# RWKV and mLSTM float32 products of 64 rows and 128 columns, cut into 64x64 quarters of the TensorE array

## The chip, the core and the metric

The kernel runs on one core of one Trainium2 chip. The metric is the device time of one execution in microseconds, less is better. A core has five engines that each work through their own instructions in order: TensorE (PE; its weight loads are listed as PEld), VectorE (DVE), ScalarE (ACT), GpSimd (POOL) and SyncE (SP, which issues the DMAs here).

TensorE multiplies a stationary operand (rows times columns of the array, at most 128x128) with a stream of columns. A product whose operands have 64 rows uses one row half of the array, and a result of 64 partitions one column half; the first is set by the partitions that the operands lie on, the second by the partitions of the result.

## The reference

The reference is a block of an RWKV-7 part beside an mLSTM part with a feed-forward part behind them, and then two layers of attention, on 1024 tokens of width 1024 in float32. The change touches the first block alone, cut here to what matters:

```python
def rwkv7_group(p, mu, w0, w_up_decay, a0, w_up_a, ...):
    ...
    log_w = -jax.nn.softplus(-(w0 + jnp.tanh(w_lo) @ w_up_decay)) - 0.5
    a = jax.nn.sigmoid(a0 + a_lo @ w_up_a)
    ...
    y = rwkv7_scan(r_h, heads(decay), k_h, v_h, -kk, kk * a_h)
    # per step: sa = S a_t;  S = S * w_t + sa b_t + v_t k_t;  y = S r_t

def mlstm_chunkwise(q, k, v, ig, logf):
    ...
    s = jnp.einsum('bhtd,bhsd->bhts', qc, kc) * d
    num = jnp.einsum('bhts,bhsv->bhtv', s, vc) + sc[..., None] * jnp.einsum('bhtd,bhdv->bhtv', qc, C)
    ...
    C = dec[..., None, None] * C + jnp.einsum('bhs,bhsd,bhsv->bhdv', w_s, kc, vc)
```

RWKV has 8 heads of 64 channels, the mLSTM 4 heads of 64 key channels and 128 value channels.

## The kernel before

Most of the time goes to the projections: products of 128 rows, 128 columns and a stream of 512 (`gemm`, `proj`, `out_half`), where each weight and each activation is split into a high and a low part (whi and wlo; act, and yh and yl) and three products are added. They are called the big products below. They run on TensorE from the start to the end, and the small work of RWKV and of the mLSTM is laid between them.

RWKV runs over 8 units of 128 tokens. Each unit has an element part (`rw_elem`), a preparation (`rw_prep`), a chain over two chunks of 64 tokens (`rw_chain`) and an output part (`rw_out`). Two heads share 128 partitions: head pair hp has one head on partitions 0 to 63 and the other on 64 to 127, H[0] and H[1] in the code.

- In `rw_elem` two up-projections with 64 rows (the weights lie in `wup`, the first on partitions 0 to 63, the second on 64 to 127) make four results of 128 partitions each, in a tile tagged e: uw from tw, and ua from L (tile ML).
- In `rw_prep` the products of BK (stationary) and AR (stream) make the score tiles. For each of two groups g two result tiles tagged m, `apm[0]` and `apm[1]`, are filled, one for each row half hh, with four products each. VectorE then masks them to AA and AM. From AA a triangular inverse is built up over levels: products GD with Y make Z (VectorE), products XD with Z and ZD with X make the next Y and X (ScalarE).
- In `rw_chain` the tile P takes 64x64 products of S, RH, UV with AR, TT, BT and AM.

The mLSTM runs over 8 blocks of 128 tokens (`ml_block`). The score products (K of a head stationary, Q the stream, both in the tile QK) go to pst and are multiplied with the decay DT to SD; the state products (Q stationary, the state C the stream) go to pq and are scaled by ScalarE to NUM. Both are done for i = 0 and 1, the row halves, with two products each; all these result tiles are tagged p. Blocks 0 to 3 take their tiles from a pool with one slot, blocks 4 to 7 from a pool with two (`psl` in `block1` and `rest`). The tiles m have two slots.

All products are issued by the helper `mm` (L186) and all transposes by `tr` (L189). The order on each engine is not that of the code: a scheduler lays it out when the program is built, by priorities and by when a slot of a pool is free. On top of that RWKV and mLSTM groups are tied to the big products. `collect` gathers a part's TensorE work into groups, a new one beginning after each instruction of another engine, and `pace` orders the last instruction of group i before the big product number start + i*n:

```python
    def pe(self, inst):
        if self.grp is not None:
            if self.brk:
                self.grp.append(inst)
```

For the mLSTM n is 12 in both halves (NM and NCC).

Of the kernel before, what the change touches and what calls it, by code (L numbers as in the profile page):

```python
# [17 lines left out]
ALU = mybir.AluOpType  # L18
# [12 lines left out]
NG = 6  # L31
PA = 56, 1, 48, 1
BF, BL = 0, 100
CDEC = -0.5 * math.exp(-0.5)


# [92 lines left out]
class Kern:  # L129
# [562 lines left out]
    def rwkv(self, R, gR, gK, gV, gL, yd):  # L692
# [14 lines left out]
        k["cdec"] = self.t(rc, [128, 1], "cdec")  # L707
        nc.vector.memset(k["cdec"], CDEC)
        k["ka"] = self.t(rc, [128, 8], "ka")
# [59 lines left out]
    def rw_elem(self, R, u, gR, gK, gV, gL):  # L769
        nc = self.nc  # L770
        re, r2, r3, pe_ = R["re"], R["r2"], R["r3"], R["pse"]
        kc = self.rk
        gp = nc.gpsimd
        t0 = 128 * u

        def load(g, M):
            nc.sync.dma_start(M, g[:, :, t0:t0 + 128])

        L = self.t(re, [128, 2, 128], "ML")
        load(gL, L)  # L780
        tw = self.t(re, [64, 128], "tw")
        self.act(tw, L[0:64, 0], AF.Tanh)
        sg = self.t(r3, [128, 128], "sg")
        self.act(sg, L[:, 1], AF.Tanh, scale=0.5)
        self.ts(sg, sg, 0.5, 0.5)
        CUM = self.t(re, [128, 4, 128], "CUM")
        A = self.t(re, [128, 4, 128], "A")
        uw = self.t(pe_, [128, 4, 128], "e")
        for hp in range(4):
            self.mm(uw[:, hp], kc["wup"][0:64, hp * 128:hp * 128 + 128], tw)  # L790
        for hp in range(4):
            self.act(CUM[:, hp], uw[:, hp], AF.Tanh, bias=kc["wa0"][:, hp:hp + 1], scale=0.5)
        ua = self.t(pe_, [128, 4, 128], "e")
        for hp in range(4):
            self.mm(ua[:, hp], kc["wup"][64:128, hp * 128:hp * 128 + 128], L[64:128, 0])
        for hp in range(4):
            self.act(A[:, hp], ua[:, hp], AF.Tanh, bias=kc["wa0"][:, 4 + hp:5 + hp], scale=0.5)
        cdec = CDEC
        lw = self.t(re, [128, 4, 128], "t1")
        self.act(lw, CUM, AF.Identity, bias=kc["cdec"], scale=cdec)  # L800
        fl = lambda x: x.rearrange("p a b -> p (a b)")
        nc.vector.tensor_tensor_scan(fl(CUM), fl(kc["msk"]), fl(lw), 0.0, op0=ALU.mult, op1=ALU.add)
        ch = lambda x: x.rearrange("p a (c t) -> p a c t", t=64)
        E1 = self.t(re, [128, 4, 2, 65], "E1")
        nc.vector.memset(E1[:, :, :, 0:1], 1.0)
        self.act(E1[:, :, :, 1:65], ch(CUM), AF.Exp)
        EN = CUM
        self.act(EN, CUM, AF.Exp, scale=-1.0)
        EC = self.t(r3, [128, 2, 4], "EC")
        nc.vector.tensor_copy(EC.rearrange("p c a -> p a c"), E1[:, :, :, 64])  # L810
        Kx = self.t(re, [128, 4, 128], "MK", bufs=2)
        load(gK, Kx)
        KA = self.t(re, [128, 4, 128], "KA")
        SQ = self.t(re, [128, 4, 128], "t1")
        for hp in range(4):
            self.act(KA[:, hp], Kx[:, hp], scale=self.par("k_k", hp))
        self.act(SQ, KA, AF.Square)
        ss = self.t(pe_, [128, 512], "e")
        for hp in range(4):
            self.mm(ss[:, 2 * hp:2 * hp + 2], SQ[:, hp], kc["hsel"])  # L820
        sv = self.t(re, [128, 8], "sv")
        self.ts(sv, ss[:, 0:8], 1e-24, op0=ALU.max)
        rn = self.rsqrt(re, sv, "rn")
        rnb = self.t(re, [128, 8, 64], "t1")
        self.act(rnb, rn[:, :, None].to_broadcast([128, 8, 64]))
        bc = self.t(pe_, [128, 4, 128], "e")
        for hp in range(4):
            self.tr(bc[:, hp], rnb[:, 2 * hp:2 * hp + 2].rearrange("p a b -> p (a b)"), self.ident)
        self.tt(KA, KA, bc)
        AR = self.t(r2, [128, 4, 2, 128], "AR")  # L830
        BK = self.t(re, [128, 4, 4, 64], "BK")
        self.tt(AR[:, :, :, 0:64], ch(KA), E1[:, :, :, 0:64])

        self.stt(KA, A, 1.0, KA, op0=ALU.add, op1=ALU.mult)
        self.stt(BK[:, :, 1:3, :], ch(KA), -0.5, ch(EN), op0=ALU.mult, op1=ALU.mult)
        K2 = self.t(re, [128, 4, 128], "t1")
        for hp in range(4):
            self.act(K2[:, hp], A[:, hp], AF.Identity, bias=kc["ka"][:, 4 + hp:5 + hp], scale=kc["ka"][:, hp:hp + 1])
        self.tt(K2, K2, Kx)
        self.tt(BK[:, :, 0:4:3, :], ch(K2), ch(EN), eng=gp)  # L840
        Rx = self.t(re, [128, 4, 128], "MK", bufs=2)
        load(gR, Rx)
        self.tt(AR[:, :, :, 64:128], ch(Rx), E1[:, :, :, 1:65], eng=gp)
        V = self.t(re, [128, 4, 128], "V")
        load(gV, V)
        RK = A
        for hp in range(4):
            self.act(RK[:, hp], Rx[:, hp], scale=self.par("r_k", hp))
        self.tt(RK, RK, K2)
        bp = self.t(pe_, [128, 4, 128], "e")  # L850
        self.mm(fl(bp), kc["bones"], fl(RK))
        BON = self.t(r3, [128, 4, 128], "BON")
        self.tt(BON, bp, V)
        return dict(AR=AR, BK=BK, V=V, BON=BON, EC=EC, sg=sg)

    def rw_prep(self, R, U):

        nc = self.nc
        rx, r2, psm = R["rx"], R["r2"], R["psm"]
        kc = self.rk  # L860
        gp = nc.gpsimd
        AR, BK, V = U["AR"], U["BK"], U["V"]
        am = kc["am"]
        H = [slice(0, 64), slice(64, 128)]
        fl2 = lambda x: x.rearrange("p a b -> p (a b)")
        AA = self.t(rx, [128, 8, 2, 64], "AA")
        AM = self.t(r2, [128, 8, 2, 64], "AM")
        for g in range(2):
            apm = [self.t(psm, [128, 4, 128], "m") for _ in range(2)]
            for h2 in range(2):  # L870
                for c in range(2):
                    for hh in range(2):
                        self.mm(apm[hh][:, h2 * 2 + c], fl2(BK[H[hh], 2 * g + h2, 2 * c:2 * c + 2, :]),
                                AR[H[hh], 2 * g + h2, c, :])
            for T_, o in ((AA, 0), (AM, 64)):
                for hh in range(2):
                    h0 = hh * 4 + 2 * g
                    self.tt(T_[:, h0:h0 + 2].rearrange("p a c t -> p (a c) t"), apm[hh][:, :, o:o + 64],
                            am[:, None, o:o + 64].to_broadcast([128, 4, 64]))
# [47 lines left out]
        for h in range(8):  # L927
            hh, hp = h // 4, h % 4
# [217 lines left out]
    def ml_block(self, tb, mc, mx, my, psm, G, gQ, gW, gO, yd):  # L1146
        nc = self.nc
        bmd, TK, DEC, trik = (G[n] for n in ("bmd", "TK", "DEC", "trik"))
        C = G["C"]
        t0 = tb * 128  # L1150
        ts_ = slice(t0, t0 + 128)
        QK = self.t(my, [128, 4, 128], "QK")
# [14 lines left out]
        DT = self.t(mx, [128, 4, 128], "DT")  # L1167
# [6 lines left out]
        for j in range(2):  # L1174
# [2 lines left out]
        self.tt(KW, pk.rearrange("p j (h d) -> p (j h) d", d=64),  # L1177
                TK[:, tb, 1, :, None].to_broadcast([128, 4, 64]))
        SD = self.t(mx, [128, 4, 128], "SD")
        for i in range(2):  # L1180
            pr = slice(i * 64, i * 64 + 64)
            pst = self.t(psm, [128, 2, 128], "p")
            for h2 in range(2):
                self.mm(pst[:, h2], QK[pr, 2 + h2], QK[pr, h2])
            self.stt(SD[:, i:4:2], pst, 0.125, DT[:, i:4:2], op0=ALU.mult, op1=ALU.mult)
        NUM = self.t(mx, [128, 4, 130], "NUM")
        for i in range(2):
            pr = slice(i * 64, i * 64 + 64)
            pq = self.t(psm, [128, 2, 130], "p")
            for h2 in range(2):  # L1190
                self.mm(pq[:, h2, 0:129], QK[pr, h2], C[pr, h2, 0:129])
            for h2 in range(2):
                h = h2 * 2 + i
                self.act(NUM[:, h, 0:129], pq[:, h2, 0:129], scale=TK[:, tb, 3, h:h + 1])
        Cn = self.t(mc, [128, 2, 130], "C", bufs=2)
        pcs = self.t(psm, [128, 2, 130], "p")
        for h in range(4):
            h2, i = h // 2, h % 2
            self.mm(pcs[i * 64:i * 64 + 64, h2, 0:129], KW[:, h], V1[:, h, 0:129])
        for h in range(4):  # L1200
            h2, i = h // 2, h % 2
            pr = slice(i * 64, i * 64 + 64)
            self.stt(Cn[pr, h2, 0:129], C[pr, h2, 0:129], DEC[pr, h, tb:tb + 1], pcs[pr, h2, 0:129])
        for h2 in range(2):
            pn = self.t(psm, [128, 2, 130], "p")
            for i in range(2):
                self.mm(pn[:, i, 0:129], SD[:, h2 * 2 + i], V1[:, h2 * 2 + i, 0:129])
            self.tt(NUM[:, 2 * h2:2 * h2 + 2, 0:129], NUM[:, 2 * h2:2 * h2 + 2, 0:129], pn[:, :, 0:129], ALU.add)
        G["C"] = Cn

        den = self.t(mx, [128, 4, 1], "den")
        self.stt(den, NUM[:, :, 128:129], -1.0, NUM[:, :, 128:129], op0=ALU.mult, op1=ALU.max)
        self.tt(den, den, TK[:, tb, 2, :, None], ALU.max)
        nc.vector.reciprocal(den, den)
        HN = self.t(mx, [128, 4, 128], "HN")
        self.tt(HN, NUM[:, :, 0:128], den.to_broadcast([128, 4, 128]))
        SQ = self.t(mx, [128, 4, 128], "th")
# [7 lines left out]
        for h in range(4):  # L1225
            self.tr(ph[:, h], HN[:, h], self.ident)
        YO = self.t(mx, [128, 4, 128], "SD")
        for h in range(4):
# [488 lines left out]
```

## Time and profile before

| | |
|---|---|
| time, median of 3 runs | 3477.56 us (3473.36 to 3477.97) |
| time of the profiled execution | 3473.78 us |
| its span | 3471.8 us |
| TensorE busy | 3364.5 us, 97% of the span |
| mean granted TensorE clock | 0.989 |
| VectorE, ScalarE, GpSimd busy | 59%, 46%, 20% |

The span runs from the first to the last instruction of the profiled execution. Busy times of matrix products are unions of instructions that overlap in the pipeline, so the time from one start to the next tells more than the duration of one. In the timeline a row is a run of equal instructions: its start, the time from its start to the end of its last instruction, and the count. A float32 product of one row in the instruction order is two passes in the trace, and a transpose is one.

### The profile page before, as it was taken

Reading aid. Unit: us, or ns where it says so; the run is one execution under the profiler, and the core shown is the slowest. Engines: PE = TensorE matmul, PEld = TensorE weight load, DVE = VectorE, ACT = ScalarE, POOL = GpSimd, SP = SyncE. Lnnn points to the kernel's source line nnn. Section 1 sums busy time; section 2 is a strip of 40 time slices with the busy share of each in tenths; the row PEclk is TensorE's granted clock in tenths of the full one; section 3 lists DMA queues with packets and bytes.
Section 4 is the critical chain, followed back from the end, with each engine's and each line's share of the span. In section 5 each row is a group of like instructions: output and inputs, shape, how many; then the busy total and the mean of one; then the engine's idle time right before and its main releaser. Section 6 shows DMA issues by size and latency. Waiting matters only on the chain.

```text
span 3471.8 us, 51104 instructions
## 1 busy us (share of the span) xinstructions
PE 3364.5 (97%) x18820; PEld 2720.0 (78%) x18820; DVE 2043.1 (59%) x4223; ACT 1607.7 (46%) x3242; POOL 703.4 (20%) x601
## 2 busy tenths in 40 slices
PE   8999999989999999999999999999999999999998
PEld 6777777767777777778888878888778888788886
DVE  7777767656655754577666762224777567712335
ACT  5477766654433433345555652123355556621232
POOL 2212222222222222241111111111321111111111
PEclk9999999999999999999999999999999999999999
DMA  5433232223333323332212122113432121211124
GB/s 159 155 119 106 92 112 77 64 81 103 113 106 96 124 93 92 93 118 84 59 50 64 54 78 64 44 49 121 153 92 58 50 64 50 81 59 52 50 74 140
DMA packets 196986, 303.51 MB, mean 87 GB/s; under 512 B 22976, under 2 KB 65600, under 8 KB 196736
## 3 DMA queue, kind: packets, MB, share of 16 engines
q1 hardware_dynamic: 196736, 300.25, 28.0%
q8 instruction: 148, 2.42, 0.3%
q14 instruction: 102, 0.84, 0.1%
HBM read 244.41 MB, written 38.98 MB: 82 GB/s over the span
## 4 chain that ended last, share of the span: by engine, by line
PE 50%; DVE 2%; ACT 2%; issue 1%; DMA 1%; SPq 1%; POOL 0%; DVEq 0%; ACTq 0%; POOLq 0%
PE p L186 30%; PE acc L186 10%; PE o L186 3%; PE t L189 3%; PE S L186 3%; DMA qw<-qf 1%; ACT whi L166 1%; DVE qf L172 1%; SPq L1374 0%; ACT dd L168 0%; PE d L186 0%; DVE wlo L172 0%; ACT ph L166 0%; DVE dd L1458 0%; DVE yt L172 0%
## 5 line engine op out<-in xcount | busy, mean ns | idle before, releaser
L186 PE MATMUL p<-act,whi 128*128 128x512 f32 x5824 | 1888.2, 401 | 24.0 <-ACT act L166 13.6
L186 PEld LDWEIGHTS p<-act,whi 128*128 128x128 f32 x5824 | 1084.4, 189 | 256.8 <-ACT act L166 14.2
L186 PE MATMUL p<-act,wlo 128*128 128x512 f32 x2912 | 1160.1, 400 | 4.3 <-DVE wlo L172 4.2
L172 POOL TENSOR_TENSOR wlo<-wraw,whi 128x512 fp32r<-128x512 f32 (+1 forms) x366 | 502.5, 1373 | 1945.2 <-ACT whi L166 1672.5
L166 ACT ACTIVATE whi<-wraw 128x512 fp32r<-128x512 f32 x732 | 424.4, 620 | 762.7 <-PE p L186 310.8
L186 PEld LDWEIGHTS p<-act,wlo 128*128 128x128 f32 x2912 | 551.0, 189 | 125.8 <-DVE wlo L172 9.3
L172 DVE TENSOR_TENSOR wlo<-wraw,whi 128x512 fp32r<-128x512 f32 x366 | 284.9, 780 | 258.0 <-ACT whi L166 257.1
L168 ACT ACTIVATE dd<-dd,nm 128x256 f32<-128x256 f32 (+7 forms) x256 | 171.1, 669 | 108.0 <-DVE nm L1458 106.2
L166 ACT ACTIVATE th<-p 128x512 f32<-128x512 f32 x96 | 56.5, 588 | 306.5 <-PE p L186 286.0
L166 ACT ACTIVATE ph<-t 128x384 fp32r<-128x384 f32 (+1 forms) x248 | 135.4, 557 | 121.8 <-PE t L189 117.3
L172 DVE TENSOR_TENSOR pl<-t,ph 128x384 fp32r<-128x384 f32 (+1 forms) x248 | 156.3, 637 | 50.1 <-ACT ph L166 47.2
L183 DVE SCALAR_TENSOR_TENSOR th<-th,acc 128x512 f32<-128x512 f32 x64 | 44.0, 688 | 223.8 <-ACT th L166 223.6
L177 POOL TENSOR_SCALAR rx<-rd 128x128 f32<-128x128 f32 x128 | 70.8, 561 | 475.4 <-PE t L189 253.6
L189 PE MATMUL t<-c_ident,dd 128*128 128x128 f32 x900 | 151.8, 274 | 1.1 <-ACT dd L168 0.8
L172 DVE TENSOR_TENSOR xs<-xs,d 128x512 f32<-128x512 f32 x132 | 88.6, 685 | 103.6 <-PE d L186 102.3
L186 PE MATMUL o<-ph,V 128*128 128x256 f32 (+1 forms) x532 | 132.0, 280 | 1.6 <-ACT ph L166 1.6
L186 PE MATMUL o<-pl,V 128*128 128x256 f32 (+1 forms) x532 | 129.0, 289 | 1.0 <-DVE pl L172 0.9
L1458 DVE CUSTOM_DVE_ANT_0 dd<-S,strip 128x512 f32<-128x512 f32 (+3 forms) x160 | 91.7, 587 | 53.3 <-PE t L189 30.0
L189 PEld LDWEIGHTS t<-c_ident,dd 128*128 128x128 f32 x900 | 107.1, 140 | 11.1 <-ACT dd L168 2.0
L186 PE MATMUL d<-gl,whi 128*128 128x512 f32 x264 | 107.4, 407 | 4.9 <-DVE gl L172 4.9
L186 PEld LDWEIGHTS o<-ph,V 128*128 128x128 f32 x532 | 98.1, 189 | 14.8 <-ACT ph L166 4.3
L186 PE MATMUL d<-gh,whi 128*128 128x512 f32 x264 | 105.3, 412 | 4.3 <-ACT gh L166 3.0
(408 smaller groups left out, 5062.5 us busy)
## 6 DMA issues: line engine op xcount, KB each, us to landing
wraw<-in_w_in SPq DMA_DIRECT2D x332, 256.0 KB, 2.7
wraw<-in_w_up SPq DMA_DIRECT2D x176, 256.0 KB, 2.6
wraw<-in_w_out SPq DMA_DIRECT2D x96, 256.0 KB, 3.2
wraw<-in_w_dn SPq DMA_DIRECT2D x88, 256.0 KB, 2.6
pT<-stage SPq DMA_DIRECT2D x52, 256.0 KB, 3.4
qw<-qf SPq DMA_DIRECT2D x160, 64.0 KB, 2.0
xd<-xs SPq DMA_DIRECT2D x32, 256.0 KB, 3.2
yd<-yt SPq DMA_DIRECT2D x32, 256.0 KB, 2.3
```

Source lines behind the costliest of these rows:

```text
L166: return self.nc.scalar.activation(out, in_, func, scale=scale, **kw)
L168: return self.nc.scalar.activation(out, in_, func, bias=bias, scale=scale, **kw)
L172: (eng or self.nc.vector).tensor_tensor(out, a, b, op=op)
L177: (eng or self.nc.vector).tensor_scalar(out, a, s1, None, op0=op0)
L183: return self.nc.vector.scalar_tensor_tensor(out, a, s, b, op0=op0, op1=op1, **kw)
L186: return self.pe(self.nc.tensor.matmul(out, lhsT, rhs, start=start, stop=stop, **kw))
L189: return self.pe(self.nc.tensor.transpose(out, in_, ident))
L1458: nc.vector.tensor_tensor_reduce(dd[:, o:o + w], sps[:, :w], strip[:, o:o + w], -1.0, init, ALU.add, ALU.min, nm)
```

## The change

The four kinds of products with 64 rows and 128 stationary columns are each made as two products with 64 columns, so that each uses one quarter of the array. A quarter is a pair of a row half and a column half. In `rw_prep` and in `ml_block` the quarters are issued in the order of QUADS: two opposite ones, then the other two. In `rw_elem` the row half is given, and the two column halves follow each other. In `ml_block` the two result tiles of the score products, and of the state products, are now taken together ahead of the products, and the instructions that read them come behind all products; before, tile and reader of i = 0 came ahead of those of i = 1.

```diff
@@ -31,6 +31,7 @@
 NG = 6
 PA = 56, 1, 48, 1
 BF, BL = 0, 100
+QUADS = (0, 0), (1, 1), (0, 1), (1, 0)
 CDEC = -0.5 * math.exp(-0.5)
 
 
@@ -787,12 +788,16 @@
         A = self.t(re, [128, 4, 128], "A")
         uw = self.t(pe_, [128, 4, 128], "e")
         for hp in range(4):
-            self.mm(uw[:, hp], kc["wup"][0:64, hp * 128:hp * 128 + 128], tw)
+            for q in range(2):
+                o = hp * 128 + q * 64
+                self.mm(uw[q * 64:q * 64 + 64, hp], kc["wup"][0:64, o:o + 64], tw)
         for hp in range(4):
             self.act(CUM[:, hp], uw[:, hp], AF.Tanh, bias=kc["wa0"][:, hp:hp + 1], scale=0.5)
         ua = self.t(pe_, [128, 4, 128], "e")
         for hp in range(4):
-            self.mm(ua[:, hp], kc["wup"][64:128, hp * 128:hp * 128 + 128], L[64:128, 0])
+            for q in range(2):
+                o = hp * 128 + q * 64
+                self.mm(ua[q * 64:q * 64 + 64, hp], kc["wup"][64:128, o:o + 64], L[64:128, 0])
         for hp in range(4):
             self.act(A[:, hp], ua[:, hp], AF.Tanh, bias=kc["wa0"][:, 4 + hp:5 + hp], scale=0.5)
         cdec = CDEC
@@ -869,8 +874,8 @@
             apm = [self.t(psm, [128, 4, 128], "m") for _ in range(2)]
             for h2 in range(2):
                 for c in range(2):
-                    for hh in range(2):
-                        self.mm(apm[hh][:, h2 * 2 + c], fl2(BK[H[hh], 2 * g + h2, 2 * c:2 * c + 2, :]),
+                    for hh, q in QUADS:
+                        self.mm(apm[hh][H[q], h2 * 2 + c], BK[H[hh], 2 * g + h2, 2 * c + q, :],
                                 AR[H[hh], 2 * g + h2, c, :])
             for T_, o in ((AA, 0), (AM, 64)):
                 for hh in range(2):
@@ -1177,21 +1182,23 @@
         self.tt(KW, pk.rearrange("p j (h d) -> p (j h) d", d=64),
                 TK[:, tb, 1, :, None].to_broadcast([128, 4, 64]))
         SD = self.t(mx, [128, 4, 128], "SD")
+        pst = [self.t(psm, [128, 2, 128], "p") for _ in range(2)]
+        for h2 in range(2):
+            for i, q in QUADS:
+                pr, o = slice(i * 64, i * 64 + 64), slice(q * 64, q * 64 + 64)
+                self.mm(pst[i][o, h2], QK[pr, 2 + h2, o], QK[pr, h2])
         for i in range(2):
-            pr = slice(i * 64, i * 64 + 64)
-            pst = self.t(psm, [128, 2, 128], "p")
-            for h2 in range(2):
-                self.mm(pst[:, h2], QK[pr, 2 + h2], QK[pr, h2])
-            self.stt(SD[:, i:4:2], pst, 0.125, DT[:, i:4:2], op0=ALU.mult, op1=ALU.mult)
+            self.stt(SD[:, i:4:2], pst[i], 0.125, DT[:, i:4:2], op0=ALU.mult, op1=ALU.mult)
         NUM = self.t(mx, [128, 4, 130], "NUM")
+        pq = [self.t(psm, [128, 2, 130], "p") for _ in range(2)]
+        for h2 in range(2):
+            for i, q in QUADS:
+                pr, o = slice(i * 64, i * 64 + 64), slice(q * 64, q * 64 + 64)
+                self.mm(pq[i][o, h2, 0:129], QK[pr, h2, o], C[pr, h2, 0:129])
         for i in range(2):
-            pr = slice(i * 64, i * 64 + 64)
-            pq = self.t(psm, [128, 2, 130], "p")
-            for h2 in range(2):
-                self.mm(pq[:, h2, 0:129], QK[pr, h2], C[pr, h2, 0:129])
             for h2 in range(2):
                 h = h2 * 2 + i
-                self.act(NUM[:, h, 0:129], pq[:, h2, 0:129], scale=TK[:, tb, 3, h:h + 1])
+                self.act(NUM[:, h, 0:129], pq[i][:, h2, 0:129], scale=TK[:, tb, 3, h:h + 1])
         Cn = self.t(mc, [128, 2, 130], "C", bufs=2)
         pcs = self.t(psm, [128, 2, 130], "p")
         for h in range(4):
```

In the order of instructions the rows of TensorE below show the products by name of result tile (m_1786 and so on), operands and shape of the result; the numbers of tiles differ between the two programs. p_... with act and whi or wlo are big products.

First place, TensorE in the preparation of RWKV unit 1, the first group of products of AR and BK. Before:

```order
L186 MATMUL m_1786<-AR_1663,BK_1664 128x128 x4
L186 MATMUL p_4325<-act_103,wlo_4316 128x512
L186 MATMUL p_4325<-act_103,whi_4315 128x512
L186 MATMUL p_4325<-act_104,whi_4315 128x512
L186 MATMUL p_4325<-act_103,wlo_4316 128x512
L186 MATMUL P_1689<-RH_1698,TT_1579 64x64 x8
L186 MATMUL m_1787<-AR_1663,BK_1664 128x128 x4
```

And now:

```order
L187 MATMUL m_1818<-AR_1695,BK_1696 64x128 x8
L187 MATMUL p_4453<-act_103,wlo_4444 128x512
L187 MATMUL p_4453<-act_103,whi_4443 128x512
L187 MATMUL p_4453<-act_104,whi_4443 128x512
L187 MATMUL p_4453<-act_103,wlo_4444 128x512
L187 MATMUL P_1721<-RH_1730,TT_1603 64x64 x8
L187 MATMUL m_1819<-AR_1695,BK_1696 64x128 x8
```

The tile of row half 0 (m_1786, now m_1818) still has all its products together, and that of row half 1 (m_1787, now m_1819) comes behind four big products and a step of the chain; four products have become eight.

Second place, TensorE in the preparation of unit 4, the second group. Before:

```order
L186 MATMUL P_5352<-S_5380,AR_2792 64x64 x8
L186 MATMUL e_5542<-A_5455,c_bones_1113 128x512
L186 MATMUL m_5603<-AR_5520,BK_5521 128x128 x4
L186 MATMUL m_5604<-AR_5520,BK_5521 128x128 x4
L186 MATMUL p_5169<-act_104,whi_5159 128x512
```

And now:

```order
L187 MATMUL p_5335<-act_104,whi_5325 128x512
L187 MATMUL m_5747<-AR_5656,BK_5657 64x128 x2
L187 MATMUL m_5748<-AR_5656,BK_5657 64x128 x2
L187 MATMUL m_5747<-AR_5656,BK_5657 64x128
L187 MATMUL m_5748<-AR_5656,BK_5657 64x128
L187 MATMUL m_5747<-AR_5656,BK_5657 64x128
L187 MATMUL m_5748<-AR_5656,BK_5657 64x128
```

Here the two tiles, and so the two row halves, now alternate; the alternation goes on until each has its eight products. Before, the four of one half were followed by the four of the other.

Third place, TensorE in the triangular inverse of unit 3, from the last products of X with ZD to the first of the next Y with GD. Before:

```order
L186 LDWEIGHTS ZD_1132
L186 MATMUL m_2593<-X_490_2566,ZD_1132 128x64
L186 MATMUL p_4787<-act_103,whi_4777 128x512
L186 MATMUL p_4787<-act_104,whi_4777 128x512
L186 MATMUL p_4787<-act_103,wlo_4778 128x512
L186 MATMUL p_4787<-act_103,whi_4777 128x512
L186 MATMUL p_4787<-act_104,whi_4777 128x512
L186 MATMUL p_4787<-act_103,wlo_4778 128x512
L186 MATMUL p_4787<-act_103,whi_4777 128x512
L186 MATMUL p_4787<-act_104,whi_4777 128x512
L186 LDWEIGHTS GD_1128
```

And now:

```order
L187 MATMUL m_2654<-Z_491_2643,XD_1130 128x64
L187 LDWEIGHTS ZD_1132
L187 MATMUL m_2665<-X_490_2638,ZD_1132 128x64
L187 LDWEIGHTS ZD_1132
L187 MATMUL m_2665<-X_490_2638,ZD_1132 128x64
...
L187 LDWEIGHTS GD_1128
L187 MATMUL m_2681<-Y_495_2674,GD_1128 128x64
```

The eight big products between the two steps have moved elsewhere, and so have four that stood between the products of Z and those of X.

## Rows read from the trace of the kernel before

**Rows 1.** The page's head: busy us, share of the span, instructions; granted clock in tenths.
```profile
span 3471.8 us, 51104 instructions
PE 3364.5 (97%) x18820; PEld 2720.0 (78%) x18820; DVE 2043.1 (59%) x4223; ACT 1607.7 (46%) x3242; POOL 703.4 (20%) x601
PEclk9999999999999999999999999999999999999999
```

**Rows 2.** Windows: stretch, its us, busy us of each engine, clock, DMA share, GB/s.
```profile
100.00:900.00 800.00, 753.78 (x6280) 585.64 (x6280) 549.43 (x1176) 502.89 (x998) 182.39 (x134) 0.98 0.33 100
900.00:3400.00 2500.00, 2462.48 (x11885) 2018.32 (x11884) 1375.62 (x2815) 1038.43 (x2133) 485.18 (x441) 1.00 0.26 79
```

**Rows 3.** Groups of TensorE by shape: passes, busy us, mean ns, idle before them.
```profile
L186 PE MATMUL m<-AR,BK 64*128 64x128 f32 x256 | 33.4, 285 | 2.5 <-DVE BK L183 2.5
L186 PE MATMUL p<-C,QK 64*128 64x129 f32 x64 | 10.7, 297 | 0.4 <-DVE SD L183 0.3 <-ACT NUM L166 0.2
L186 PE MATMUL p<-QK 64*128 64x128 f32 x64 | 10.6, 297 | 1.2 <-DVE SD L183 0.9 <-DVE KW L172 0.3
L186 PE MATMUL e<-tw,wup 64*128 64x128 f32 x64 | 9.6, 285 | 0.0
L186 PE MATMUL e<-ML,wup 64*128 64x128 f32 x64 | 9.5, 286 | 0.7 <-ACT CUM L168 0.7
```

**Rows 4.** Timeline of TensorE, groups in one row half: start, us, instructions.
```profile
205.61 0.39 PE L186 MATMUL p<-act,wlo 128*128 128x512 f32 x1
205.84 0.62 PE L186 MATMUL p<-act,whi 128*128 128x512 f32 x2
206.30 0.40 PE L186 MATMUL p<-act,wlo 128*128 128x512 f32 x1
206.63 0.71 PE L186 MATMUL p<-C,QK 64*128 64x129 f32 x4
...
225.79 1.16 PE L186 MATMUL m<-AR,BK 64*128 64x128 f32 x8
```

**Rows 5.** Timeline of TensorE, halves or quarters that alternate or don't.
```profile
228.00 1.14 PE L186 MATMUL P<-RH,TT 64*64 64x64 f32 x16
...
245.05 0.69 PE L186 MATMUL P<-UV,BT 128*64 128x64 f32 x16
...
250.78 0.69 PE L186 MATMUL P<-S,AR 64*64 64x64 f32 x32
...
451.49 1.16 PE L186 MATMUL m<-AR,BK 64*128 64x128 f32 x16 [2.47 <-DVE BK L183]
...
457.10 1.71 PE L186 MATMUL m<-AR,BK 64*128 64x128 f32 x16
...
778.94 0.72 PE L186 MATMUL p<-QK 64*128 64x128 f32 x8
...
822.28 0.66 PE L186 MATMUL p<-V,KW 128*64 128x129 f32 x8
```

**Rows 6.** Waits of TensorE from 100 to 900 us: total us, times, longest.
```profile
PE p L186 <- ACT act L166: 4.7, 3, 2.7
PE m L186 <- DVE Z L172: 3.8, 3, 2.8
PE m L186 <- ACT XD L166: 3.7, 6, 1.4
PE e L189 <- POOL YS L172: 3.2, 1, 3.2
...
PE m L186 <- DVE BK L183: 2.5, 1, 2.5
...
PE m L186 <- ACT ZD L166: 1.9, 5, 0.8
```

**Rows 7.** Windows with two of the longer waits, columns as in rows 2.
```profile
449.00:458.00 9.00, 6.53 (x52) 4.53 (x51) 6.08 (x13) 2.56 (x8) 1.65 (x1) 0.81 0.31 88
489.00:501.00 12.00, 8.38 (x62) 5.79 (x61) 4.18 (x7) 9.92 (x24) 2.43 (x2) 0.72 0.55 165
```

**Rows 8.** Instructions on tile Y: duration ns min/median/max, first and last start.
```profile
L166 ACT ACTIVATE Y<-m x32: 574/597/615, 182.3 to 718.0; 128x512 f16<-128x512 f32 x32
```

## The prediction

> **What bounds the kernel now.** I read the page's head first, then the windows, then the list of TensorE's groups, and only then single stretches. TensorE is busy for 97% of the span at a mean granted clock of 0.989 of full speed [rows 1]; the reader is to see that no other engine comes near it. The windows show where it is not full: from 100 to 900 us, where the RWKV and mLSTM work runs between the big products, it is busy 753.8 of 800 us, and from 900 us to 3400 us it is busy 2462.5 of 2500 us [rows 2]. All the changed products lie in the first of these stretches. The list of TensorE's groups gives their whole size: 33.4 us for the RWKV products of AR and BK, 9.6 and 9.5 us for the two up-projections, 10.7 and 10.6 us for the two mLSTM products of QK [rows 3], together 73.8 us, 2.1% of the span. That is the most the change can touch. The list of waits shows what fills the other 46 us of that window: many short waits for VectorE and ScalarE, none above 3.2 us, of which those of the RWKV preparation (Z, XD, BK, ZD) make up 11.9 us [rows 6].
>
> **How long such a group takes, and why.** A float32 product is two passes in the trace: the order has 128 products of AR and BK, the trace 256 [rows 3]. Eight passes of 64 rows and 128 columns that all sit in one row half take 1.16 us, four take 0.71 us [rows 4], so 0.11 us a pass, one behind the other, with 0.26 us around them. Where the two row halves alternate, sixteen such passes take the same 1.16 us, and eight take 0.72 us [rows 5]: two halves run side by side, 0.11 us a pair. Between these, sixteen passes that alternate at first and then don't take 1.71 us. The 64-column passes show the same thing at half the size: sixteen in one quarter take 1.14 us, sixteen that alternate between the two column halves 0.69 us, and thirty-two that go through all four quarters in turn 0.69 us as well [rows 5]. So four quarters can run at once, and this already happens in the kernel before. The rate is then four quarter passes in the time of one.
>
> That decides the change by its order, not by its shape. A product cut into two quarters is worth nothing if only these two quarters follow each other: two quarters side by side take what one half took. It is worth a half where quarters of both row halves alternate and before they did not. The instruction order says where that is. The two result tiles of a group come from a pool that frees its slots at different times, so nearly everywhere all products of the first tile, which is one row half, stand together, with other work before those of the second tile. In RWKV units 1, 2, 3, 5, 6 and 7 this holds before and after, 24 groups of four products. In unit 0 the halves alternated before already. Only the second group of unit 4 changes from two runs of one half to quarters in turn. The mLSTM blocks 0 to 3 have one slot for both tiles, and the up-projections use one row half by construction. In blocks 4 to 7, which have two slots, the first pair alternates before too (eight passes in 0.72 us, [rows 5]).
>
> **The sum.** (1) The groups in one row half. The price of a group after isn't in the trace; the nearest rows are eight passes of 64 columns and a 129-wide stream, four pairs in 0.66 us [rows 5], against 0.71 us for four half passes [rows 4]. With four more pairs at 0.11 us that makes 1.10 us against 1.16 us. What is saved is the shorter first weight load. Thus 24 RWKV groups at 0.06 us, 1.4 us; 16 up-projection groups of four products at 0.06 us, 1.0 us; 32 mLSTM groups of two products at 0.05 us, 1.6 us. The bounds: nothing saved (a group then lasts as before), or, if the columns didn't run side by side, twice the passes (a rival below). I take 4.0 us. (2) Unit 4's second group: two runs of 1.16 us before, then eight rounds of four quarters, 1.10 us by the same row; it had run as sixteen passes in 1.71 us [rows 5], so 0.6 to 1.2 us, of which I take 0.9. (3) Changes of the array's division. A big product starts 0.23 us after the one before it, and the first narrow one 0.33 us after a big one [rows 4], so a change costs about 0.1 us. Over the order of products the division changes 323 times before and 312 times after, since the changed groups now share a division with their 64-by-64 neighbours: 1.1 us. (4) Instructions: 256 products become 512, or 512 more passes. At thirty-two passes in 0.69 us [rows 5] one pass can be issued in 0.02 us, far under 0.11 us a pair, so I cost this at nothing; were it not hidden, 512 times 0.02 would be 10 us, and that is the bound. Together some 6 us come off TensorE's own work.
>
> (5) The order around them. The scheduler places everything between about 120 and 900 us anew, on all five queues; the work after that stands in the same order on TensorE. RWKV keeps its places among the big products, because its groups are tied to their count. In an mLSTM block the two score products now count as one group, and the two state products as one, so a block has 8 paced groups for 10; block 3 ends after 1050 big products for 1080, block 7 after 2235 for 2328. Nobody waits for that: the first reader of those results stands behind 1248 big products. What matters is how far a group stands from the work that it waits for. Counting in the order the groups that stand within two big products of the group they follow, I find 39 before and 42 after. Fewer in the mLSTM (13 before, 7 after), more in the RWKV preparation (26 and 35). The worst are in unit 3, where Z, X and the next Y products now follow each other with no big product between, while ScalarE takes 0.6 us to move one result to Y [rows 8]; before there were four and eight big products of 0.23 us between them. Such a wait costs between 0 and the 1.4 us that is the longest one for XD [rows 6]. The net three places, at 1 us, and the extra wait in unit 3 are put at 3 us; the ends are 4 us gained (six fewer mLSTM places at 0.7 us) and 13 us lost (nine RWKV places at 1.4 us). So 6 saved less 3 gives 3 us. VectorE and ScalarE do the same instructions, and no transfer is added.
>
> The profiled execution took 3473.8 us (span 3471.8 us [rows 1]), 3.8 us under the median of 3477.6 us. The sum gives 3470.8 us for an execution like the profiled one, and 3474.5 us for a median like the one shown; I forecast 3474.5 us.
>
> **Rivals.** (a) The dependent groups stand too close. This is the mechanism of (5) at its full price. Nine more RWKV places at 1.4 us are 13 us, and such idle time also halves the clock: in the 9 us that begin with the 2.5 us wait for BK the granted clock is 0.81, and in the 12 us with the wait for act it is 0.72 [rows 7]. Two more such stretches cost 9 times 0.19 and 12 times 0.28, 5 us. Less the 6 us saved, 3489 us. It decides as soon as TensorE's waits in this window grow from 46 to over 60 us. For it: no big product between Z, X and Y in unit 3. Against: the mLSTM places, and that the other places in RWKV are nearly unchanged.
>
> (b) The waits shrink with the work. The 6 us are kept and the new order takes 6 us off the 46 us of waits, the mLSTM's places above all: 3466 us. For it: TensorE is 94% busy in this window [rows 2], so what is saved there mostly moves the end, and one clock drop less is worth 2 to 3 us.
>
> (c) The four quarters overlap everywhere, as the new code is written. Then half of the 73.8 us less the parts that alternated before, some 30 us, would go: 3447 us. Against it stands the order.
>
> (d) Quarters of one row half don't overlap. Some 220 products, all but those that alternate, would take two passes of 0.11 us more each: 48 us, 3526 us. The sixteen passes that alternate between column halves in 0.69 us against 1.14 us in one quarter speak against it [rows 5], though these have 128 rows and not 64; the thirty-two in four quarters have 64. The Trainium skill's "TensorE: Matmul & The Clock Gate", Part 3 on packing small matmuls, speaks for it: a weight load overlaps with running products only if the row group differs, and here it is the same. The trace disagrees, since by that rule the passes with all rows and alternating column halves could not take 0.69 us.
>
> **How the numbers follow.** The measurement of this kernel can tell about 0.2%, 7 us, from no change. The forecast, some saving between none and 7 us, gets 0.49. Faster by more: (b) 0.26 and (c) 0.03. Slower by more: (a) 0.19 and (d) 0.03. Around the forecast the saving may be 6 us and the waits 4 us better or 9 us worse, which gives 3467 to 3481 us. The range for 8 in 10 reaches into (b) and up to (a), 3463 to 3488 us, and leaves out (c) and (d).
>
> **What would show it.** In the trace after, eight products of one row half of AR and BK, sixteen passes, should stand in the timeline at about 1.10 us, and at 2.0 us or more if (d) is right. Unit 4's second group should take 1.10 us for thirty-two passes. The busy time of the m, e and p groups together should fall by only a few us from 73.8; a fall by 30 is (c). TensorE's waits between 100 and 900 us should be 45 to 55 us; above 60 us is (a), under 42 us (b). The forecast is wrong if the time moves by more than 7 us either way.

## The result and the profile after

The changed kernel takes 3499.2 us (median of 4 runs, 3497.5 to 3506.2) against 3476.7 us for the kernel before (4 runs beside it, 3473.4 to 3478.0). The ratio is 1.0069, 95% interval 1.0054 to 1.0085: slower by some 23 us. I had forecast 3474.5 us and a range up to 3488.

The page's head of the kernel after, to be read beside [rows 1]:

```profile
span 3497.5 us, 52144 instructions
PE 3373.5 (96%) x19332; PEld 2721.6 (78%) x19332; DVE 2053.5 (59%) x4223; ACT 1603.6 (46%) x3242; POOL 701.7 (20%) x601
PEclk9989999999999999999999999999999999999999
```

TensorE is busy 9 us longer, and the span is 26 us longer. The 512 more passes are there (19332 for 18820), and the busy times of the other engines move by some 10 us or less, with the same instructions. The clock has a dip that was not there, in the third slice. The windows, with the columns of [rows 2]; the last two are the dip and the 19 us ahead of it:

```profile
100.00:900.00 800.00, 740.94 (x6709) 570.32 (x6707) 541.90 (x1152) 491.57 (x984) 176.99 (x131) 0.96 0.32 98
900.00:3400.00 2500.00, 2459.01 (x11862) 2014.99 (x11861) 1380.90 (x2824) 1036.46 (x2131) 482.50 (x438) 0.99 0.25 78
...
232.00:249.00 17.00, 17.00 (x110) 13.20 (x107) 9.61 (x29) 1.22 (x2) 0.00 (x0) 0.50 0.01 3
213.00:232.00 19.00, 15.25 (x178) 11.48 (x176) 16.19 (x38) 14.77 (x31) 3.66 (x3) 1.00 0.39 114
```

From 100 to 900 us TensorE now stands idle for 59.1 us; it was 46.2 us. In the dip it runs without a gap, at 0.50 of full speed, 1.2 GHz.

The cut products themselves, by shape (columns of [rows 3]):

```profile
L187 PE MATMUL m<-AR,BK 64*64 64x128 f32 x512 | 33.4, 292 | 0.0
L187 PE MATMUL p<-C,QK 64*64 64x129 f32 x128 | 10.7, 283 | 0.2 <-ACT NUM L167 0.2
L187 PE MATMUL p<-QK 64*64 64x128 f32 x128 | 10.0, 281 | 1.3 <-DVE SD L184 1.3
L187 PE MATMUL e<-tw,wup 64*64 64x128 f32 x128 | 9.1, 275 | 0.6 <-DVE BON L173 0.3 <-DVE YQ L173 0.3
L187 PE MATMUL e<-ML,wup 64*64 64x128 f32 x128 | 9.0, 276 | 1.2 <-ACT CUM L169 1.2
```

Twice the passes, 72.2 us for 73.8. Single groups in the timeline answer to [rows 4] and [rows 5] (start, us, instructions):

```profile
206.18 0.65 PE L187 MATMUL p<-QK 64*64 64x128 f32 x8
...
211.32 0.66 PE L187 MATMUL p<-C,QK 64*64 64x129 f32 x8
...
231.66 1.60 PE L187 MATMUL m<-AR,BK 64*64 64x128 f32 x16
...
386.60 1.09 PE L187 MATMUL m<-AR,BK 64*64 64x128 f32 x16
...
469.58 1.10 PE L187 MATMUL m<-AR,BK 64*64 64x128 f32 x32
```

Sixteen quarter passes of one row half take 1.09 us where eight half passes took 1.16, and thirty-two through all four quarters take 1.10 us. The group at 231.66 runs into the dip, so it takes 1.60 us: a busy time that grows where the clock falls is no longer work.

The waits of TensorE from 100 to 930 us (total us, times, longest), beside [rows 6]. First the wait for HN before, which stands far down that list, then the head of the list after:

```profile
PE p L189 <- DVE HN L172: 1.5, 2, 1.2
```

```profile
PE p L190 <- DVE HN L173: 18.6, 4, 8.6
PE m L187 <- ACT XD L167: 5.0, 7, 1.3
```

XD, which I had watched, is 1.3 us up. HN is new at the head of the list. HN is the normalised output of an mLSTM block: VectorE and ScalarE make it from NUM and the last product of V and SD, and TensorE transposes it. Here is the same block in both timelines, first before, then after:

```profile
797.33 0.61 PE L186 MATMUL p<-V,SD 128*128 128x129 f32 x4
...
810.24 0.63 PE L189 MATMUL p<-c_ident,HN 128*128 128x128 f32 x4 [0.29 <-DVE HN L172]
```

```profile
801.04 0.61 PE L187 MATMUL p<-V,SD 128*128 128x129 f32 x4
...
804.24 0.39 PE L187 MATMUL p<-act,wlo 128*128 128x512 f32 x1
813.27 1.09 PE L190 MATMUL p<-c_ident,HN 128*128 128x128 f32 x4 [8.64 <-DVE HN L173]
```

From the product to the transpose it is 12 to 13 us in both. Before, 40 big products stood in between and covered it; now 13 do, and TensorE stands for 8.64 us with everything else behind the transpose in its queue. VectorE's timeline of these 8 us shows the chain (start, us):

```profile
804.21 0.41 DVE L173 TENSOR_TENSOR NUM<-NUM,p 128x258 f32<-128x258 f32 x1
...
805.26 0.69 DVE L173 TENSOR_TENSOR HN<-NUM,den 128x512 f32<-128x512 f32 x1
806.65 0.69 DVE L1227 TENSOR_REDUCE va<-th 128x4 f32<-128x512 f32 x1 [0.69 <-ACT th L167]
...
812.43 0.69 DVE L173 TENSOR_TENSOR HN<-HN,mry 128x512 f32<-128x512 f32 x1
```

Between these steps VectorE also does other work (gl and wlo of the big products, cv). The 12 us are thus the chain together with what stands between its steps in VectorE's order; what it takes without that was not tried.

**Where the 23 us are.** I compared the stretch from big product 386 to big product 2500, counted from 0 in each trace, which holds the same work in each kernel. "Idle" is time in which no product of TensorE runs, "at half" the time in which it works at the clock of 1.2 GHz, added up from the trace's records; what is left, with the time at half counted half, is work at full clock. One profiled execution each, us; those of e1, f1 and e8 lie 5, 7 and 9 us above the medians of their runs, those of e4, e5 and f2 8, 8 and 5 us below, the others within 4 us:

```
kernel                            stretch   idle   at half   work
before                             840.3    51.9    37.2    769.9
after                              863.9    68.1    66.1    762.8
e1  after, ten groups              853.4    56.7    77.3    758.1
e2  before, eight groups           857.8    62.4    55.2    767.7
e3  RWKV quarters only             854.9    57.1    61.3    767.2
e4  mLSTM quarters, ten groups     845.6    55.6    51.3    764.3
e5  after, groups 15 apart         845.5    53.1    71.7    756.6
e6  up-projection quarters only    849.7    55.4    48.3    770.2
f1  quarters in the old order      850.9    57.0    60.4    763.7
f2  halves in the order of e6      857.7    54.2    71.2    767.9
f4  halves in the new order        862.5    65.7    59.7    767.0
e7  AR,BK quarters only            840.1    52.4    37.3    769.0
e8  halves alternate               845.8    60.8    50.1    759.9
e9  quarters alternate             840.3    60.3    40.3    760.0
```

Work fell by 7.1 us, idle time rose by 16.2, and 28.9 us more at half the clock cost 14.5. The sum is the 23.6 us of the stretch. The last column isn't exact: the same uncut products count 767.0 to 769.9 us (before, e2, f2, f4), the same cut ones 756.6 to 763.7 us (after, e1, e5, f1). In the pairs of equal order the cut saves 6.2 us (f1 against before) and 4.2 us (after against f4).

### The profile page after: what moved, and what is told of

It reads as the page before. It is cut to its first block, busy times and chain, and to the rows that moved or that the text cites. A ratio compares the mean times of both kernels' runs of the same rounds, so it can differ in the third digit from the quotient of the medians.

```text
span 3497.5 us, 52144 instructions
## 1 busy us (share of the span) xinstructions
PE 3373.5 (96%) x19332; PEld 2721.6 (78%) x19332; DVE 2053.5 (59%) x4223; ACT 1603.6 (46%) x3242; POOL 701.7 (20%) x601
## 4 chain that ended last, share of the span: by engine, by line
PE 51%; DVE 2%; ACT 2%; issue 1%; DMA 0%; POOL 0%; SPq 0%; DVEq 0%; ACTq 0%; POOLq 0%
PE p L187 31%; PE acc L187 10%; PE o L187 3%; PE t L190 3%; PE S L187 3%; ACT whi L167 0%; DMA qw<-qf 0%; PE d L187 0%; DVE wlo L173 0%; ACT dd L169 0%; DVE qf L173 0%; DVE dd L1465 0%; DVE yt L173 0%; ACT ph L167 0%; SPq L1381 0%
## 5 line engine op out<-in xcount | busy, mean ns | idle before, releaser
L187 PE MATMUL p<-act,whi 128*128 128x512 f32 x5824 | 1895.8, 403 | 28.9 <-ACT act L167 12.9
```

The source lines that it names most:

```text
L187: return self.pe(self.nc.tensor.matmul(out, lhsT, rhs, start=start, stop=stop, **kw))
```

## The experiments

Two theories stood against each other: the cut products cost time themselves (issue, changes of the array's division, loads), or the order that came with them does. In the expectations the first is theory Q; the second is theory P where it is the pacing of the mLSTM alone, and theory O where it is any new order. Each ratio below is to the kernel before in runs on the same chip, with its 95% interval.

**The pacing of the mLSTM.** e1 is the changed kernel with ten paced groups in a block, as before: a new group begins at each pair of heads, in the score products (shown) and in the state products.

```diff
         for h2 in range(2):
+            self.brk = True
             for i, q in QUADS:
```

> The changed kernel with ten paced groups per mLSTM block again: the score products and the state products count as two groups each, by a break at each h2. Theory P (pacing): the eight groups bring the last transposes of a block (HN) 25 to 90 big products nearer to the start, TensorE waits for HN, and that is some 21 of the 23 us; then 3472 to 3486 us, and the waits for HN between 100 and 930 us fall from 18.6 us to under 3 us. Theory Q (the quarters themselves cost: drains, or a lower clock because narrow products keep the array less busy): no change, 3495 to 3503 us.

3485.8 us, 1.0020 (1.0007 to 1.0032): some 17 us of the loss are gone. The time is at the upper end of theory P's range, and the wait for HN is above the 3 us that it allowed:

```profile
PE p L190 <- DVE HN L173: 4.6, 3, 2.7
```

e2 is the other way round: the kernel before, its products uncut, with the pairs of groups joined to eight.

```diff
             self.stt(SD[:, i:4:2], pst, 0.125, DT[:, i:4:2], op0=ALU.mult, op1=ALU.mult)
+            self.brk = i == 1
...
                 self.act(NUM[:, h, 0:129], pq[:, h2, 0:129], scale=TK[:, tb, 3, h:h + 1])
+            self.brk = i == 1
```

> The kernel before with its products untouched, and only the paced groups of the mLSTM merged from ten to eight per block. Theory P: slower than before by 15 to 25 us, 3492 to 3502 us, with TensorE waiting 12 to 20 us for HN. Theory Q: as before, 3473 to 3481 us.

3492.1 us, 1.0045 (1.0029 to 1.0061). No product is cut here, and both the loss and the wait are there, as theory P had it:

```profile
PE p L189 <- DVE HN L172: 15.1, 4, 7.7
```

e5 keeps the eight groups of the changed kernel and sets them 15 big products apart for 12 (NM and NCC), so that a block again spans 120.

> The changed kernel with eight groups, but a step of 15 big products for 12, so that a block spans 120 of them as before. Theory P: most of the loss goes, 3473 to 3488 us, HN waits under 4 us. Theory Q: 3495 to 3503 us.

3488.3 us, 1.0021 (1.0005 to 1.0037), just past theory P's range (3488 us, and under 4 us for HN):

```profile
PE p L190 <- DVE HN L173: 4.2, 2, 2.6
```

Two different edits give the same time; what they share is the block's length in big products. So joining the groups, which comes with moving the readers behind all products, is a cause of its own and the largest one found, 15 to 17 us by e1, e2 and e5.

**Parts of the change alone.** e3 has the quarters in `rw_elem` and `rw_prep` only, e4 in `ml_block` only (with ten groups), e6 in `rw_elem` only, e7 in `rw_prep` only; each edit is its part of the diff.

> Quarters in the RWKV parts alone; the mLSTM as before, with ten groups. Theory P: 3470 to 3484 us, since nothing of the pacing changes. Theory Q: RWKV has 192 of the 256 cut products, so most of the loss stays, 3490 to 3500 us.

3491.5 us, 1.0038 (1.0024 to 1.0052). This is theory Q's range, and theory P failed: 13 us are lost with ten groups and a wait for HN of 3.5 us.

> Quarters in the mLSTM alone, with ten paced groups per block; RWKV as before. If the pacing was all that the mLSTM part cost (theory P): 3474 to 3481 us. If cutting itself costs there (theory Q): 3485 us and more.

3487.6 us, 1.0016 (1.0001 to 1.0030), again where theory Q put it and not P, though the ten runs spread from 3473 to 3496 us.

> Quarters in the two up-projections alone (64 of the 256 cut products). The RWKV quarters cost 13 us together. Theory O (it is the new order around them, which holds the clock at 1.2 GHz for some 17 us near 205 us): either of the two parts alone may bring it or not, and where the page shows no such stretch the time is 3474 to 3481 us. Theory Q (the cut products themselves): a third of the loss, 3481 to 3484 us, whatever the clock.

3488.4 us, 1.0026 (1.0016 to 1.0036), though its up-projections went from 9.6 and 9.5 to 9.1 and 9.4 us. Both theories failed here: O forecast 3474 to 3481 us where no long stretch at half the clock stands near 205 us, and the profile has none (its longest is 10.2 us, at 378 us); Q forecast at most 3484 us.

> Quarters in the RWKV preparation alone (128 of the 256 cut products). Theory O: 3474 to 3481 us if no long stretch at 1.2 GHz stands near 205 us, some 9 us more if one does. Theory Q: two thirds of the RWKV loss, 3485 to 3488 us.

3479.6 us, 0.9995 (0.9983 to 1.0006), as theory O had it, and the only part without a loss:

```profile
L187 PE MATMUL m<-AR,BK 64*64 64x128 f32 x512 | 31.0, 280 | 2.9 <-POOL BK L173 1.6 <-DVE BK L184 1.3
```

The parts don't add up. e1 holds the quarters of e3 and of e4 and costs 7 us, where these cost 13 and 6 us apart; the gap of 12 us is clear of the three intervals, which together leave some 8 us open. (`rw_elem` and `rw_prep`, 9 and -2 us apart and 13 together in e3, differ by less than their intervals.) In e3 idle time rose by 5 us, work fell by 3 and 24 us more ran at half the clock. A cost of the quarters would add; an order that each edit lays anew need not.

**The order held.** In f4 the products are uncut, but TensorE's first 5600 products are held in the order of the changed kernel; f1 is the reverse, all quarters, held in the order of the kernel before (each product's two quarters in its place). f2 holds uncut products in the order of e6. A list of numbers gives the order, and each product is tied behind the one ahead of it in that list; nothing holds VectorE and ScalarE.

```diff
+    def force(self):
+        at, last = 0, None
+        for x in ORDER.split():
...
+                for i in self.allpe[at]:
+                    if last is not None:
+                        self.behind(i, last)
+                    last = i
```

> The products of the kernel before, uncut, with TensorE held in the order of the changed kernel. Theory O: as slow as the changed kernel or slower by the work that it saves, 3495 to 3510 us. Theory Q: 3474 to 3484 us.

3501.4 us, 1.0071 (1.0057 to 1.0085): uncut products in the new order are as slow as the changed kernel (1.0069), by the same wait, as theory O had it.

```profile
PE p L256 <- DVE HN L239: 20.2, 6, 6.7
```

> All 256 products cut into two quarters each, in the place of the old product: TensorE's first 5600 products are held in the order of the kernel before. Theory O (the loss is the order, by waits and clock; the cut products themselves save some 6 us of work): 3468 to 3478 us. Theory Q (the cut products cost): 3485 us and more.

3481.2 us, 1.0016 (1.0007 to 1.0025). This lies between the ranges of both theories. The wait for HN is 1.6 us, as before, and work is 6.2 us down; but idle is 5 us up, and one stretch of 20.5 us at 601 us runs at half the clock. Here are its window from 100 to 900 us, its two largest waits and that for HN:

```profile
100.00:900.00 800.00, 749.48 (x6733) 576.39 (x6731) 544.26 (x1156) 499.21 (x991) 178.79 (x133) 0.96 0.33 100
```

```profile
PE m L253 <- DVE Z L239: 4.4, 3, 2.8
PE m L253 <- ACT XD L233: 4.1, 5, 1.4
...
PE p L256 <- DVE HN L239: 1.6, 2, 1.3
```

What holding the order costs by itself isn't known: no run holds the kernel before in its own order.

> The products of the kernel before, uncut, with TensorE held in the order that the cut up-projections alone led to (that version took 3488 us). Theory O: the loss is there without any cut product, 3483 to 3492 us. Theory Q: 3474 to 3481 us.

3497.8 us, 1.0061 (1.0047 to 1.0075), above theory O's range and slower than e6 with the same order on TensorE. So the order of TensorE alone gives the time no closer than 0.35%, 12 us. The table shows where f2 is slower: not in idle time, but in 23 us more at half the clock, above all a stretch of 17.1 us at 229 us and one of 20.5 us at 608 us. Ahead of the second, TensorE waits 1.1 us for ZD; f1 has the same wait ahead of its stretch of 20.5 us, and e6 and the kernel before don't have it. VectorE, which nothing holds, makes ZD behind a step on nh that waits for GpSimd in f1 and f2, and ahead of it in the other two. First f1, VectorE and then TensorE, then the kernel before:

```profile
598.29 0.75 DVE L250 SCALAR_TENSOR_TENSOR nh<-xs,pk,p 128x512 f32<-128x512 f32 x1 [0.51 <-POOL act L239]
598.95 1.38 DVE L239 TENSOR_TENSOR ZD<-c_idc,m 64x512 bf16<-64x512 f32 x2
...
600.38 0.41 PE L253 MATMUL m<-X,ZD 128*128 128x64 bf16 x8 [1.12 <-DVE ZD L239]
```

```profile
596.96 1.38 DVE L172 TENSOR_TENSOR ZD<-c_idc,m 64x512 bf16<-64x512 f32 x2
598.37 0.75 DVE L183 SCALAR_TENSOR_TENSOR nh<-xs,pk,p 128x512 f32<-128x512 f32 x1
...
598.39 0.41 PE L186 MATMUL m<-X,ZD 128*128 128x64 bf16 x8
```

That this wait brings the stretch at half the clock is read from its place, and was not tested.

**Is there anything in quarters at all?** By the trace before it is the alternation of the row halves that brings the rate. e8 has the uncut products of AR and BK in alternation, each tied behind the last; e9 the same with quarters.

```diff
-                        self.mm(apm[hh][:, h2 * 2 + c], fl2(BK[H[hh], 2 * g + h2, 2 * c:2 * c + 2, :]),
+                        i = self.mm(apm[hh][:, h2 * 2 + c], fl2(BK[H[hh], 2 * g + h2, 2 * c:2 * c + 2, :]),
                                 AR[H[hh], 2 * g + h2, c, :])
+                        if h2 + c + hh:
+                            self.behind(i, last)
+                        last = i
```

> The kernel before with products of 64 rows and 128 columns, but those of AR and BK ordered so that the row halves alternate, as in unit 0. If the alternation and not the shape decides the rate, sixteen passes stand in 1.16 us everywhere, the m<-AR,BK group falls from 33.4 to some 21 us busy, and the time is 3462 to 3476 us; if the first tile's slot is held for nothing meanwhile, as before or slower, 3476 to 3485 us.

> The kernel before, with the products of AR and BK alone made as quarters, and each held behind the one before it in the order of QUADS, so that all 16 groups alternate between the row halves and between the column halves. e8 did the same with uncut products: their busy time fell from 33.4 to 24.2 us, and 7.0 us of waits for GD came in their place. If the rate is set by the alternation of the row halves alone, a group of 32 quarter passes takes what 16 half passes took (1.10 to 1.16 us), the busy time of this group is again 23 to 26 us, TensorE waits for GD as in e8, and the time is 3477 to 3486 us, 0.999 to 1.002 of the kernel before. If cutting brings a rate of its own where the quarters alternate, the busy time falls to 12 to 18 us and the time to about 3470 us (0.997).

e8: 3480.4 us, 1.0002 (0.9990 to 1.0014). e9: 3478.4 us, 1.0002 (0.9993 to 1.0011). e9 came out as forecast; e8 in its second range, but by a wait for GD and not by the reason given there. Both have the gain in the products and give it back as a wait. The group and the largest wait of e8:

```profile
L186 PE MATMUL m<-AR,BK 64*128 64x128 f32 x256 | 24.2, 304 | 1.1 <-DVE BK L183 1.1
```

```profile
PE m L186 <- DVE GD L172: 7.0, 4, 2.7
```

And of e9:

```profile
L187 PE MATMUL m<-AR,BK 64*64 64x128 f32 x512 | 24.7, 286 | 2.2 <-POOL BK L173 1.6 <-DVE va L180 0.3 <-DVE AM L173 0.2
```

```profile
PE m L187 <- DVE GD L173: 9.6, 5, 3.1
```

24.2 us uncut and 24.7 us cut, for 33.4 before: the quarters add nothing to the rate that alternating row halves have. Work is 10 us less, idle time 8 to 9 us more. GD, which VectorE makes further down the same chain, cost 0.9 us of waits in the kernel before. In the order of these two the second tile's products no longer stand apart from the first's, so less work lies between the products and GD; that this alone makes the wait is read from the order, and was not tested. No version that ran beats the kernel before; e7, e8 and e9 equal it.

## Why the prediction was wrong

- **Terms (1) to (4), right in the main.** One row half 1.09 us (1.10 forecast), unit 4's second group 1.10 us (1.10), all together 7.1 us less work, or 4.2 and 6.2 us in the pairs of equal order (6). The row of 1.71 us was misread: by its starts in the trace it doesn't "alternate at first", but has four single passes, then pairs between 457.65 and 457.99 us, then single ones: the run of one half begins beside the end of the other's. The term doesn't change by that. That the diff's order of quarters hardly reaches the chip, since the two tiles come free apart, held too: 33.4 us of AR and BK before and after. The issue of 512 more passes, bounded at 10 us, shows no cost: f1 has all of them and 6.2 us less work, and f4 without them is as slow as the changed kernel. How (1) to (3) share the 7.1 us was not taken apart.
- **Term (5), the step that failed**, in its words: "a block has 8 paced groups for 10; block 3 ends after 1050 big products for 1080, block 7 after 2235 for 2328. Nobody waits for that: the first reader of those results stands behind 1248 big products." I had looked for a reader behind the block, and left out the readers inside it. The shorter block has the same chain from V and SD to HN, 12 to 13 us at its longest, and fewer big products to cover it. TensorE itself waits, in order, at the transposes. e2 shows this with no other change: 1.0045.
- **Its count could not see it.** I counted groups within two big products of what they follow, some 0.5 us. A chain of 12 us needs 50 big products of 0.23 us. Counted so, in the instruction order from the last product of V and SD to the transposes of HN, the blocks 4 to 7 had 40, 48, 38 and 66, and now have 13, 36, 30 and 16. With 12 us less 13 times 0.23 us, 9 us of wait could have been worked out beforehand; the trace has 8.64. For the other three blocks the same sum gives 3.7, 5.1 and 8.3 us, and the trace has 0.02, 3.65 and 4.66: from the product to the transpose they take only 9 to 12 us, so the sum finds the place and bounds the wait, but doesn't size it.
- **The net 3 us of waits** were 12.8 us between 100 and 900 us, and 16.2 in the longer stretch. The places that I priced, Z and XD of unit 3, were not it: XD is up 1.3 us.
- **The clock** stood as a loss in rival (a) alone, with 5 us. It cost some 14 us. The rival was right in its kind (dependent groups too close, with the clock falling), and waits of 59 us against its 60 us, but its place was another, and its 3489 us were 10 short. It should have had more than a fifth of the chances, as [rows 7] shows the clock falling after waits of 2.5 us.
- **(b), (c) and (d) are out.** (b): some waits shrank (Z from 3.8 to 1.9 us), but idle time grew, by 5 us even in f1. (c): AR and BK at 33.4 us. (d): sixteen passes at 1.09 us where it asked for 2.0 us or more. By this the trace disagrees again with the Trainium skill's "TensorE: Matmul & The Clock Gate", Part 3, on packing small matmuls, where a weight load overlaps running products only if the row group differs: in the group of sixteen at 386.60 us, all in one row half, the passes start in pairs, 0.11 us from pair to pair, and the next weight loads start while such a pair runs.
- **Open.** From before to e1 and f1 a loss of 0.2% stays, with work 12 and 6 us down; in their profiles it stands in idle time (5 us each) and in time at half the clock (40 and 23 us more). Whether holding the order has a part in f1's loss, and why one order has long stretches at half the clock and another hasn't, was not settled.

## What to carry to other kernels

Where an engine works in order, price a change of order by the longest chain that leaves the engine and comes back to it: its length in us, less the time of the independent work that still stands in between. A regrouping that changes how many steps a planner counts moves whole blocks of dependent work, and can cost more than the cut saves: here 15 to 17 us against 4 to 7. Before cutting small products for the array, look whether those that can run side by side do follow each other: the same rate came from reordering uncut products, and even then 10 us less work bought nothing where the next result was not ready.

## What the runs showed that I had not expected

The clock stayed at half for 17 us in which TensorE had no idle time at all (17.00 of 17.00 us busy at 0.50). It followed 19 us at full clock with 3.75 us of gaps, the last of them 2.15 us:

```profile
228.54 0.63 PE L187 MATMUL p<-act,whi 128*128 128x512 f32 x2
231.32 0.41 PE L187 MATMUL m<-X,ZD 128*128 128x64 bf16 x8 [2.15 <-DVE ZD L173]
231.66 1.60 PE L187 MATMUL m<-AR,BK 64*64 64x128 f32 x16
```

In that stretch TensorE worked on small products and some big ones between them. e1 has two such stretches of 17.1 us, at 207 and 385 us, and f1 one of 20.5 us at 601; the kernel before, whose 2.47 us wait for BK [rows 5] cost it 3.4 us at half the clock, has none over 13.7 us ahead of the last 12 us of its span. And e6 has the same wait for ZD ahead of the same products, with the clock at 1.00 from 209 to 245 us:

```profile
228.75 0.41 PE L186 MATMUL m<-X,ZD 128*128 128x64 bf16 x8 [2.15 <-DVE ZD L172]
```

A gap of 2 us was thus followed by no fall of the clock in one order, by 3 us at half the clock in another and by 17 us in a third, with 8.5 us lost there: more than the change saved.
